# Two-sided staging buffers in a PEER gate stage, and earlier room for the row pools and the first five expert blocks

## The chip, the cores and the metric

One Trainium2 chip, one of its cores. The metric is device time in microseconds (us) of one execution. The engines of the core are TensorE (PE in the rows; PEld is its weight load), VectorE (DVE), ScalarE (ACT), GpSimd (POOL) and SyncE (SP). SP, ACT and POOL also issue DMA transfers; each issues in its own program order, so a transfer that has to wait holds back what stands behind it on that queue.

## The reference

One layer of an encoder on 1024 tokens of width 1024. The part that matters here is its last, a layer of 16384 single-neuron experts:

```python
def one_block(xb):
    ...
    eid = jnp.take_along_axis(cand_i, pos, axis=-1)
    gate = jax.nn.softmax(best_s, axis=-1)
    u = jnp.take(expert_down, eid, axis=0)
    act = jax.nn.gelu(jnp.einsum('thkd,td->thk', u, xb).astype(jnp.float32), approximate=False)
    v = jnp.take(expert_up, eid, axis=0)
    return jnp.einsum('thk,thkd->td', (gate * act).astype(v.dtype), v)
```

Each token chooses 8 x 16 experts; its result is the gated sum of their output rows. Before it stand attention, retention and two projections, behind it a last RMSNorm. All of it is float32; products on PE are made of three passes over operands split in a high and a low part.

## The kernel before

The 1024 tokens are eight tiles of 128. Five tiles (set B) go through **all** 16384 experts as dense products, in 128 blocks of 128 experts; the other three tiles (set A) fetch their chosen experts' rows with indirect DMAs (gathers).

The stages in order of time: attention and retention with the output projection; the choice of experts (to about 893 us); then the **gate stage** (lines 890 to 931); then the **dense stage** (lines 934 to 1160), to the end.

- *The gate stage* turns the choices of each of the five B tiles into a dense table. Per tile and per group of four tokens it builds two one-hot matrices (`oh` on DVE, `bo` on ACT, `ao` mostly on POOL), multiplies them on PE (`pg`), and copies the product into a staging buffer `stg` of 64 KB in each partition (DVE and ACT). Eight DMAs of 1 MB on SP's queue then store a tile's `stg` in `g_dr` in DRAM (line 930), as runs of 512 bytes. Pool `gs` holds two `stg` buffers: tiles 0, 2 and 4 use one, tiles 1 and 3 the other.
- *The dense stage* runs over the 128 blocks. For a block, `ur` (512 KB of `ut`) is loaded and split into `uh` (ACT) and `ul` (DVE) by `split_u`; `products` multiplies them with the five tiles' activations (48 matmuls into `pa`) and ACT applies the GELU (`hf`); `down` multiplies with the block's row of `g_dr` (`gt`) and splits the result into `hh` and `hl`; `up` multiplies these with the halves `vh`, `vl` of the output rows `vr` (30 matmuls into `po` per block) and `add` sums into `acc`.
- *The prologue of the dense stage* (lines 1112 to 1135) does the products of blocks 0 to 4 ahead of everything else: their loads have own buffers `first0` to `first4` in pool `pro`, and their results go to `hfirst0` to `hfirst4`. Later each `first` buffer takes that block's row of `g_dr`. Four gathers stand beside each of these five blocks.
- *The gathers* (`gather_tiles`): POOL issues an indirect DMA of 128 rows of 4 KB (512 KB) into one of five buffers `rows` in pool `gp`, and DVE reduces it against the tile's activations `xng` (line 988). `xng` is loaded over ACT's queue (line 984).

A scheduler orders the instructions of each engine when the program is built; each engine then runs its own in that order. A pool's room can be used by another pool only when every last use of the tiles in it is over. In bytes of a partition, the pools of the two stages lie as follows: `gw` with `gc` (one-hots) 26272 to 52896, `gs` 52896 to 183968 (first buffer to 118432, second from there), and, for the dense stage, `du` (`ur`, `uh`, `ul`, `vr`) 17056 to 44192, `dc` (`acc`) 44192 to 64672, `dw` (`gt`, `hh`, `hl`, `vh`, `vl`) 64672 to 115360, `pro` 122848 to 156128, `gp` 156128 to 185312. So `pro` and `gp` lie over `gs`'s second buffer, `dw` over its first.

```python
stg = pg_.tile([P, P, P], F32, name="stg")
...
for k in range(0, P, 16):
    nc.sync.dma_start(g_dr.rearrange("a b t -> b a t")[:, k:k + 16, i * P:(i + 1) * P], stg[:, k:k + 16])
```

Of the kernel before, what the change touches and what calls it, by code (L numbers as in the profile page):

```python
# [10 lines left out]
F32 = mybir.dt.float32  # L11
# [10 lines left out]
P = 128  # L22
# [3 lines left out]
DC = D // P  # L26
# [7 lines left out]
SETS = {"A": list(range(NT - NG, NT)), "B": list(range(NT - NG))}  # L34
# [6 lines left out]
FIRST = 5  # L41
# [13 lines left out]
def peer_layer(tc, ap, dbg=None):  # L55
    nc = tc.nc
    V, S, G, PE = nc.vector, nc.scalar, nc.gpsimd, nc.tensor
# [19 lines left out]
    with ExitStack() as top:  # L77
# [15 lines left out]
        x1_dr = [dram.tile([P, D], F32, name=f"x1_dr{t}") for t in range(NT)]  # L93
# [27 lines left out]
        with ExitStack() as es:  # L121
# [4 lines left out]
            ps = es.enter_context(tc.tile_pool(name="pm", bufs=1, space=PSUM))  # L126
# [207 lines left out]
            for gi, (half, nm) in enumerate(order):  # L334
# [4 lines left out]
                for c2 in range(DC // 2):  # L339
# [11 lines left out]
                    for k, tt in ks:  # L351
                        c = 2 * c2 + k
# [21 lines left out]
                for tt in range(4):  # L374
                    t = 4 * half + tt
# [20 lines left out]
        with ExitStack() as es:  # L396
# [3 lines left out]
            ps = es.enter_context(tc.tile_pool(name="aps", bufs=2, space=PSUM))  # L400
# [71 lines left out]
            def values(h, out):  # L472
                vt = vts[h]
                po = ps.tile([P, 512], F32, name="avp", bufs=1)
                for j in range(NT):
                    mm3(po, vt[:, 0, j], vt[:, 1, j], ah[j // 4][:, j % 4], al[j // 4][:, j % 4],
                        j == 0, j == NT - 1)
                    if j == 3:
                        yield
                oT = pw.tile([P, 512], F32, name="oT", bufs=1)  # L480
                S.activation(oT, po, AF.Copy)
                out.append(oT)
# [59 lines left out]
            for u in range(-2, len(units) + 1):  # L542
# [13 lines left out]
                if 0 <= u < len(units):  # L556
                    h, g, t = units[u]
# [32 lines left out]
        nB = len(SETS["B"])  # L590
        wB = nB * P
# [60 lines left out]
        with ExitStack() as es:  # L652
            ps = es.enter_context(tc.tile_pool(name="ops", bufs=2, space=PSUM))
# [25 lines left out]
            for u, (nm, i, t) in enumerate(todo):  # L679
# [4 lines left out]
                if u == 1:  # L684
                    first = weights(pw0, 0)
                if last is not None:
                    turned(ps, *last, "otp")
                    if last[0] == "A0":
                        first = first, query(pn, ps, SEGS, *first, ("pq", 1), False)
# [161 lines left out]
        def products(ps, hf, bufs, uh, ul):  # L851
            w = wB // parts
            for r in range(parts):
                cs = slice(r * w, r * w + w)
                pa = ps.tile([P, w], F32, name="pa", bufs=bufs)
                for c in range(DC):
                    mm3(pa, uh[:, c], ul[:, c], nh[:, c, cs], nl[:, c, cs], c == 0, c == DC - 1)
                S.activation(hf[:, cs], pa, AF.Gelu)  # L858
# [3 lines left out]
        with ExitStack() as es:  # L862
            pq_ = {k: es.enter_context(tc.tile_pool(name=f"swq{k}", bufs=1)) for k in (1, 2, 0)}
            pw = es.enter_context(tc.tile_pool(name="sw", bufs=2))
            ps = es.enter_context(tc.tile_pool(name="sps", bufs=2, space=PSUM))
# [23 lines left out]


        g_dr = dram.tile([P, P, wB], F32, name="g_dr")
        with ExitStack() as es:
            pc = es.enter_context(tc.tile_pool(name="gc", bufs=1))
            pw = es.enter_context(tc.tile_pool(name="gw", bufs=4))
            pg_ = es.enter_context(tc.tile_pool(name="gs", bufs=2))
            ps = es.enter_context(tc.tile_pool(name="gps", bufs=2, space=PSUM))
            iop = pc.tile([P, P, 4], BF16, name="iop")
            G.iota(iop, pattern=[[1, P], [0, 4]], base=0, channel_multiplier=0, allow_small_or_imprecise_dtypes=True)
            for i in range(nB):
                pT = ps.tile([P, 3, P], F32, name="gtp")  # L900
                for k in range(3):
                    PE.transpose(pT[:, k], selE[k][:, i].rearrange("p h k -> p (h k)"), ident)
                kT = pw.tile([P, 2, P], BF16, name="kT", bufs=1)
                V.tensor_copy(kT, pT[:, 0:2])
                gT = pw.tile([P, P], F32, name="gT", bufs=1)
                V.tensor_copy(gT, pT[:, 2])
                stg = pg_.tile([P, P, P], F32, name="stg")
                for q in range(0, P, 4):
                    o2 = pw.tile([P, 2, P, 4], BF16, name="oh")
                    V.tensor_tensor(o2, bc(iop[:, None], [P, 2, P, 4]), bc(kT[:, :, None, q:q + 4], [P, 2, P, 4]),  # L910
                                    op=ALU.is_equal)
                    oh = [o2[:, k].rearrange("p n t -> p t n") for k in range(2)]
                    bo = pw.tile([P, 4, P], F32, name="bo")
                    S.activation(bo, oh[1], AF.Copy)
                    ao = pw.tile([P, 4, P], F32, name="ao")
                    if q // 4 % 11:
                        G.tensor_tensor(ao, oh[0], bc(gT[:, q:q + 4, None], [P, 4, P]), op=ALU.mult)  # L917
                    else:
                        for j in range(4):
                            S.activation(ao[:, j], oh[0][:, j], AF.Copy, scale=gT[:, q + j:q + j + 1])  # L920
                    pg = ps.tile([P, 4, P], F32, name="pg", bufs=6)
                    for j in range(4):
                        PE.matmul(pg[:, j], bo[:, j], ao[:, j], start=True, stop=True)  # L923
                    dst, src = stg[:, :, q:q + 4], pg.rearrange("p t a -> p a t")
                    if q // 4 % 5 in (0, 2):
                        V.tensor_copy(dst, src)
                    else:
                        S.activation(dst, src, AF.Copy)
                for k in range(0, P, 16):
                    nc.sync.dma_start(g_dr.rearrange("a b t -> b a t")[:, k:k + 16, i * P:(i + 1) * P], stg[:, k:k + 16])  # L930
        early.close()


        gp = top.enter_context(tc.tile_pool(name="gp", bufs=1, side="right"))
        late = {}

        def tail(t, o):
# [65 lines left out]
        with ExitStack() as es:  # L1003
# [4 lines left out]
            acc = [pc.tile([P, D], F32, name=f"acc{i}") for i in range(nB)]  # L1008
# [21 lines left out]
            def load(a):  # L1030

                if a < P and a not in BEFORE:
                    raw[a] = pu.tile([P, DC, P], F32, name="ur", bufs=1)
                    nc.sync.dma_start(raw[a], ap["ut"][a])
# [10 lines left out]
            def split_u(a):  # L1045
                if a in raw:
                    uh = pu.tile([P, DC, P], F32R, name="uh")
                    ul = pu.tile([P, DC, P], F32R, name="ul")
                    ur = raw.pop(a)
                    S.activation(uh, ur, AF.Copy)  # L1050
                    V.tensor_tensor(ul, ur, uh.bitcast(F32), op=ALU.subtract)  # L1051
                    ready[a] = uh, ul

            def down(a):
                hf, gt = ready.pop(a), gts.pop(a)
                if isinstance(hf, tuple):
                    u, hf = hf, pu.tile([P, wB], F32, name="hf", bufs=1)
                    products(ps, hf, 2, *u)

                mark[0] = V.tensor_tensor(gt, gt, hf, op=ALU.mult).ins  # L1060

                if a >= FIRST:
                    gathers(RATE / 4)
                hh = pd.tile([P, wB], F32R, name="hh", bufs=2 * GB - 1)
                hl = pd.tile([P, wB], F32R, name="hl", bufs=2 * GB - 1)
                S.activation(hh, gt, AF.Copy)
                V.tensor_tensor(hl, gt, hh.bitcast(F32), op=ALU.subtract)
                hs[a] = hh, hl
                if a >= FIRST:
                    gathers(RATE / 4)  # L1070
# [38 lines left out]
                        add(k, t)  # L1109


            with tc.tile_pool(name="pro", bufs=1, side="right") as pp:
                first = [pp.tile([P, DC * P], F32, name=f"first{a}") for a in range(FIRST)]
                for a, ur in enumerate(first):
                    S.dma_start(ur.rearrange("p (c e) -> p c e", e=P), ap["ut"][a])
                load(FIRST)
                for a, ur in enumerate(first):
                    raw[a] = ur.rearrange("p (c e) -> p c e", e=P)
                    split_u(a)
                    ready[a] = ready[a], pp.tile([P, wB], F32, name=f"hfirst{a}")  # L1120
                    products(ps, ready[a][1], 2, *ready[a][0])
                    ready[a] = ready[a][1]
                    for _ in range(4):
                        next(gen)
                split_u(FIRST)
                load(FIRST + 1)
                values(0)
                values(1)
                for a, ur in enumerate(first):
                    gts[a] = ur[:, 0:wB]  # L1130
                    nc.sync.dma_start(gts[a], g_dr[a])
                for t, o in zip(SETS["B"], acc):
                    nc.sync.dma_start(o, x1_dr[t])
                for a in range(FIRST):
                    down(a)
            for a in range(FIRST - 1, P):
                if a >= FIRST:
                    down(a)
# [70 lines left out]
```

## Time and profile before

| | us |
|---|---|
| median of three runs | 3129.86 (3127.61 to 3130.92) |
| the profiled execution | 3130.9 |
| its span, first to last instruction | 3129.1 |
| PE busy in the span | 2850.7 (91%) |
| DVE busy | 2589.1 (83%) |
| POOL busy | 1706.6 (55%) |
| ACT busy | 1071.8 (34%) |

The profile is of one execution; 1.8 us of its time lie outside the span. Times in the rows count from the span's start. Durations of neighbouring matmuls overlap, so a count of matmuls over the time between two starts tells PE's pace better than the sum of their durations. PEclk is the granted clock of PE as a share of full speed; "DMA share" the mean busy share of the 16 DMA engines.

### The profile page before, as it was taken

What the parts mean: (1) busy time and instruction counts of PE and PEld (TensorE: products, weight loads), DVE (VectorE), ACT (ScalarE), POOL (GpSimd) and SP (SyncE); (2) the same over time, 40 slices, a digit from 0 to 9 for tenths busy, and PEclk for the clock granted to TensorE, in tenths of its full rate; (3) what the DMA queues carried; (4) which work ended last, traced back from release to release, by engine and by line L of the source; (5) the groups of instructions that cost most, each with busy time, mean ns of one, the idle gap of its engine ahead of it and who ended that gap; (6) DMA issues with size and microseconds to landing.
All of it is one profiled execution on the core that took longest, in us unless ns stands there. A gap on an engine that the chain in (4) does not pass through costs nothing.

```text
span 3129.1 us, 44717 instructions
## 1 busy us (share of the span) xinstructions
PE 2850.7 (91%) x15999; PEld 2528.5 (81%) x15999; DVE 2589.1 (83%) x4867; ACT 1071.8 (34%) x1750; POOL 1706.6 (55%) x1319
## 2 busy tenths in 40 slices
PE   8999798898978847998899898999999999999998
PEld 6888577798977637887788787898999889998997
DVE  5465587579999946898998888888999988889997
ACT  4444466422247732222223222222222222222222
POOL 3422455346559944666556556565555465655551
PEclk9999899999999978999899999999999999999999
DMA  4334955331006688877777879999999899999994
GB/s 160 110 122 134 197 115 108 123 127 37 23 18 172 176 254 308 304 275 260 280 267 249 279 273 352 330 325 325 341 328 326 298 348 326 328 331 337 330 325 169
DMA packets 327919, 742.54 MB, mean 237 GB/s; under 512 B 25872, under 2 KB 133008, under 8 KB 327696
## 3 DMA queue, kind: packets, MB, share of 16 engines
q0 software_dynamic: 123520, 419.48, 39.2%
q1 hardware_dynamic: 201584, 315.28, 30.7%
q10 hardware_dynamic: 2592, 4.93, 0.5%
q8 instruction: 126, 2.06, 0.3%
q14 instruction: 97, 0.79, 0.1%
HBM read 669.26 MB, written 70.32 MB: 236 GB/s over the span
## 4 chain that ended last, share of the span: by engine, by line
PE 27%; DVE 15%; issue 14%; POOL 8%; DMA 5%; ACT 1%; SPq 1%; POOLq 0%; DVEq 0%; ACTq 0%
POOL rows L978 6%; PE po L73 5%; PE po L75 5%; PE po L74 5%; PE pa L73 4%; PE pa L74 4%; PE pa L75 4%; DVE gacc L997 4%; DVE rows L988 2%; DVE oh L910 2%; DMA rows<-peer_u,idx 2%; DMA ur<-ut 1%; POOL ao L917 1%; DVE acc L1094 1%; SPq L930 1%
## 5 line engine op out<-in xcount | busy, mean ns | idle before, releaser
L978 POOL DMA_INDIRECT rows<-peer_u,idx x384 | 525.8, 1369 | 401.6 <-DVE act L988 236.7
L978 POOL DMA_INDIRECT rows<-peer_v,idx x384 | 470.1, 1224 | 401.7 <-DVE gacc L997 338.4
L73 PE MATMUL pa<-nThB,uh 128*128 128x320 f32 x2048 | 639.0, 312 | 54.4 <-ACT uh L1050 39.4
L75 PE MATMUL pa<-nThB,ul 128*128 128x320 f32 x2048 | 636.0, 311 | 15.3 <-DVE ul L1051 15.3
L74 PE MATMUL pa<-nTlB,uh 128*128 128x320 f32 x2048 | 636.5, 311 | 0.0
L73 PE MATMUL po<-vh,hh 128*128 128x512 f32 x1280 | 516.0, 404 | 66.1 <-DVE acc L1094 65.9
L75 PE MATMUL po<-vh,hl 128*128 128x512 f32 x1280 | 509.6, 398 | 0.0
L74 PE MATMUL po<-vl,hh 128*128 128x512 f32 x1280 | 508.3, 397 | 0.7 <-DVE vl L1083 0.7
L997 DVE SCALAR_TENSOR_TENSOR gacc<-rows,act,gacc 128x1024 f32<-128x1024 f32 x384 | 502.9, 1310 | 5.5 <-DMA rows<-peer_v,idx 4.6
L988 DVE CUSTOM_DVE_ANT_0 rows<-rows,xng 128x1024 f32<-128x1024 f32 x384 | 467.0, 1246 | 44.8 <-DMA rows<-peer_u,idx 30.1
L73 PEld LDWEIGHTS pa<-nThB,uh 128*128 128x128 f32 x2048 | 389.9, 190 | 61.0 <-ACT uh L1050 39.6
L75 PEld LDWEIGHTS pa<-nThB,ul 128*128 128x128 f32 x2048 | 389.7, 190 | 16.6 <-DVE ul L1051 16.0
L74 PEld LDWEIGHTS pa<-nTlB,uh 128*128 128x128 f32 x2048 | 390.0, 190 | 4.4
L73 PEld LDWEIGHTS po<-vh,hh 128*128 128x128 f32 x1280 | 246.8, 193 | 124.5 <-DVE acc L1094 75.1
L1082 ACT ACTIVATE vh<-vr 128x512 fp32r<-128x512 f32 x256 | 160.2, 628 | 384.4 <-PE po L75 168.0
L75 PEld LDWEIGHTS po<-vh,hl 128*128 128x128 f32 x1280 | 246.2, 192 | 55.6
L74 PEld LDWEIGHTS po<-vl,hh 128*128 128x128 f32 x1280 | 246.7, 193 | 49.1 <-DVE vl L1083 1.5
L1050 ACT ACTIVATE uh<-ur 128x1024 fp32r<-128x1024 f32 x118 | 125.2, 1061 | 371.1 <-PE pa L74 199.1
L1051 DVE TENSOR_TENSOR ul<-ur,uh 128x1024 fp32r<-128x1024 f32 x118 | 145.7, 1234 | 102.6 <-ACT uh L1050 67.5
L917 POOL TENSOR_TENSOR ao<-oh,gT 128x512 f32<-128x512 bf16 x145 | 206.9, 1462 | 22.3 <-DVE oh L910 22.3
L923 PE MATMUL pg<-ao,bo 128*128 128x128 f32 x1280 | 181.5, 289 | 41.0 <-POOL ao L917 32.3
L858 ACT ACTIVATE hf<-pa 128x320 f32<-128x320 f32 x246 | 105.7, 430 | 328.4 <-PE pa L75 300.3
(344 smaller groups left out, 5481.3 us busy)
## 6 DMA issues: line engine op xcount, KB each, us to landing
vr<-peer_v SPq DMA_DIRECT2D x256, 256.0 KB
ur<-ut SPq DMA_DIRECT2D x123, 512.0 KB
g_dr<-stg SPq DMA_DIRECT2D x40, 1024.0 KB
gt<-g_dr SPq DMA_DIRECT2D x123, 320.0 KB
wr<-w_in SPq DMA_DIRECT2D x48, 512.0 KB
wqr<-wq SPq DMA_DIRECT2D x32, 576.0 KB
kt<-dk_dr POOLq DMA_DIRECT2D x16, 512.0 KB
xr<-xT SPq DMA_DIRECT2D x24, 256.0 KB
```

What stands on the lines that cost most here:

```text
L73: PE.matmul(out, ah, bh, start=first, stop=False)
L74: PE.matmul(out, ah, bl, start=False, stop=False)
L75: PE.matmul(out, al, bh, start=False, stop=last)
L858: S.activation(hf[:, cs], pa, AF.Gelu)
L917: G.tensor_tensor(ao, oh[0], bc(gT[:, q:q + 4, None], [P, 4, P]), op=ALU.mult)
L923: PE.matmul(pg[:, j], bo[:, j], ao[:, j], start=True, stop=True)
L978: G.indirect_dma_start(out=u, out_offset=None, in_=table, in_offset=bass.IndirectOffsetOnAxis(ap=idx, axis=0))
L988: V.tensor_tensor_reduce(out=u, in0=u, in1=xn, scale=1.0, scalar=0.0, op0=ALU.mult, op1=ALU.add, accum_out=act[:, k:k + 1])
L997: V.scalar_tensor_tensor(o, v, act[:, k:k + 1], o, op0=ALU.mult, op1=ALU.add)
L1050: S.activation(uh, ur, AF.Copy)
L1051: V.tensor_tensor(ul, ur, uh.bitcast(F32), op=ALU.subtract)
L1082: S.activation(vh, vr, AF.Copy)
```

## The change

The two `stg` buffers become two pools of one buffer each: `gs0` on the left at 52896 to 118432 and `gs1` on the right at 119776 to 185312. `gs1` is closed after tile 3 (the last tile that uses it) instead of after tile 4, and the pools `gp` and `pro` are opened at once, inside the loop, together with the loads of the five `first` buffers. Those loads go from ACT's queue to SP's. `pro` is closed where its block ended before. The other pools keep their places. The core of the diff:

```diff
         g_dr = dram.tile([P, P, wB], F32, name="g_dr")
+        pros = ExitStack()
         with ExitStack() as es:
...
-            pg_ = es.enter_context(tc.tile_pool(name="gs", bufs=2))
+
+            odd = ExitStack()
+            pgs = [es.enter_context(tc.tile_pool(name="gs0", bufs=1)),
+                   odd.enter_context(tc.tile_pool(name="gs1", bufs=1, side="right"))]
...
-                stg = pg_.tile([P, P, P], F32, name="stg")
+                stg = pgs[i % 2].tile([P, P, P], F32, name="stg")
...
                 for k in range(0, P, 16):
                     nc.sync.dma_start(g_dr.rearrange("a b t -> b a t")[:, k:k + 16, i * P:(i + 1) * P], stg[:, k:k + 16])
+                if i == (nB - 2 if nB % 2 else nB - 1):
+                    odd.close()
+                    gp = top.enter_context(tc.tile_pool(name="gp", bufs=1, side="right"))
+                    pp = pros.enter_context(tc.tile_pool(name="pro", bufs=1, side="right"))
+                    firsts = [pp.tile([P, DC * P], F32, name=f"first{a}") for a in range(FIRST)]
+                    for a, ur in enumerate(firsts):
+                        nc.sync.dma_start(ur.rearrange("p (c e) -> p c e", e=P), ap["ut"][a])
         early.close()
 
 
-        gp = top.enter_context(tc.tile_pool(name="gp", bufs=1, side="right"))
...
-            with tc.tile_pool(name="pro", bufs=1, side="right") as pp:
-                first = [pp.tile([P, DC * P], F32, name=f"first{a}") for a in range(FIRST)]
-                for a, ur in enumerate(first):
-                    S.dma_start(ur.rearrange("p (c e) -> p c e", e=P), ap["ut"][a])
-                load(FIRST)
...
+            load(FIRST)
...
             for a in range(FIRST):
                 down(a)
+            pros.close()
```

Three places show how the instructions move. First SP's queue at the end of the gate stage; `g_dr<-stg` are the stores (eight a tile, 40 in all), `ur` is the load of block 5, `vr` are output rows, `first<-g_dr` the blocks' rows of the table. Before:

```order
L930 DMA g_dr<-stg 128x16x128 x32
L1034 DMA ur<-ut 128x1024
L930 DMA g_dr<-stg 128x16x128 x8
L1079 DMA vr<-peer_v 128x512 x2
L1133 DMA acc_10827<-x_dr_70 128x1024
```

Now:

```order
L934 DMA g_dr<-stg 128x16x128 x32
L941 DMA first_10405<-ut 128x1024
L941 DMA first_10406<-ut 128x1024
L941 DMA first_10407<-ut 128x1024
L941 DMA first_10408<-ut 128x1024
L941 DMA first_10409<-ut 128x1024
L934 DMA g_dr<-stg 128x16x128 x8
L1044 DMA ur<-ut 128x1024
L1089 DMA vr<-peer_v 128x512 x2
L1137 DMA first_10405<-g_dr 128x640
```

The five loads stand between the stores of tile 3 and those of tile 4, and the load of block 5 has moved from ahead of tile 4's stores to behind them.

Second ACT's order, from the gate stage's last copies on. Before:

```order
L928 ACTIVATE stg<-pg 128x128x4 x3
L1115 DMA first_10835<-ut 128x1024
L1115 DMA first_10836<-ut 128x1024
L1115 DMA first_10837<-ut 128x1024
L1115 DMA first_10838<-ut 128x1024
L1115 DMA first_10839<-ut 128x1024
L1050 ACTIVATE uh<-first_10835 128x1024
L984 DMA xng<-xn_dr_83 128x1024
L1050 ACTIVATE uh<-first_10836 128x1024
L1082 ACTIVATE vh<-vr 128x512 x2
```

Now:

```order
L932 ACTIVATE stg<-pg 128x128x4 x2
L994 DMA xng<-xn_dr_83 128x1024
L932 ACTIVATE stg<-pg 128x128x4
L1060 ACTIVATE uh<-first_10405 128x1024
L1060 ACTIVATE uh<-first_10406 128x1024
L858 ACTIVATE hfirst_10855<-pa 128x320
L1060 ACTIVATE uh<-first_10407 128x1024
```

The load of `xng` is issued ahead of the last copy, the split of block 0 right behind it, and `vh` no longer stands among the first splits.

Third DVE's order from its last copies on; `ISA rows,act` is the reduction of a gather (an `ISA act` behind each reads its sum). Before:

```order
L926 COPY stg<-pg 128x128x4 x2
L1051 TENSOR_TENSOR ul<-first_10835,uh 128x1024
L1051 TENSOR_TENSOR ul<-first_10836,uh 128x1024
L988 ISA rows,act<-rows,xng 128x1024
L988 ISA act 128x1
```

Now:

```order
L930 COPY stg<-pg 128x128x4 x2
L998 ISA rows,act<-rows,xng 128x1024
L998 ISA act 128x1
L1061 TENSOR_TENSOR ul<-first_10405,uh 128x1024
L998 ISA rows,act<-rows,xng 128x1024
L998 ISA act 128x1
L998 ISA rows,act<-rows,xng 128x1024
L998 ISA act 128x1
L1061 TENSOR_TENSOR ul<-first_10406,uh 128x1024
```

Before, two splits stood ahead of the first reduction and eight reductions between the second split and the third; now one reduction stands ahead of the first split, two more ahead of the second, and four, four, five and three ahead of those of blocks 2, 3, 4 and 5. Some 120 DVE instructions further on, and from that place on every engine, the orders before and now are the same.

## Rows read from the trace of the kernel before

**Rows 1.** Stretches: us; PE, PEld, DVE, ACT, POOL busy (count); PEclk; DMA share; GB/s.

```profile
1129.50:1169.00 39.50, 0.07 (x2) 0.06 (x1) 0.07 (x1) 1.65 (x2) 4.16 (x5) 0.56 0.98 291
1169.00:1300.00 131.00, 113.00 (x639) 105.42 (x640) 96.26 (x143) 35.77 (x57) 65.82 (x47) 0.89 0.86 307
...
1700.00:1900.00 200.00, 182.01 (x991) 162.81 (x990) 180.55 (x339) 56.03 (x84) 111.86 (x88) 0.95 0.80 280
1900.00:2100.00 200.00, 191.95 (x1070) 174.67 (x1069) 174.83 (x273) 52.02 (x84) 122.10 (x90) 0.98 0.92 330
...
2900.00:3000.00 100.00, 100.00 (x564) 91.28 (x563) 89.89 (x97) 27.56 (x44) 52.69 (x44) 1.00 0.92 327
```

**Rows 2.** Waits from 1129 to 1230 us: total, times, longest.

```profile
PE pa L73 <- ACT uh L1050: 39.4, 1, 39.4
POOL rows L978 <- DMA vr<-peer_v: 35.3, 1, 35.3
...
PE pa L75 <- DVE ul L1051: 14.7, 1, 14.7
```

**Rows 3.** The chain that ended last, across the gap: start, us, what.

```profile
1151.56 10.80 DMA g_dr<-stg
...
1162.75 4.69 DMA first<-ut
...
1170.57 16.77 DMA xng<-xn_dr
```

**Rows 4.** SP's queue in order of time: start, us, what was issued.

```profile
1087.59 24.40 SPq L930 DMA_DIRECT2D g_dr<-stg  x8
...
1130.17 24.96 SPq L930 DMA_DIRECT2D g_dr<-stg  x8
1155.17 5.17 SPq L1079 DMA_DIRECT2D vr<-peer_v  x2
```

**Rows 5.** Short stretches around the gap, columns as in rows 1.

```profile
1112.00:1121.00 9.00, 7.59 (x56) 6.67 (x56) 9.00 (x10) 7.80 (x16) 8.31 (x7) 1.00 0.71 197
1121.00:1130.00 9.00, 7.01 (x51) 5.84 (x49) 6.69 (x8) 5.07 (x9) 7.30 (x6) 1.00 0.00 1
1130.00:1140.00 10.00, 0.00 (x0) 0.00 (x0) 0.00 (x0) 0.14 (x1) 0.00 (x0) 0.71 0.96 288
...
1190.00:1200.00 10.00, 0.00 (x0) 0.00 (x0) 7.03 (x13) 0.00 (x0) 8.17 (x7) 0.50 0.73 234
```

**Rows 6.** PE in order of time; in brackets the idle time before.

```profile
1168.95 0.63 PE L73 MATMUL pa<-nThB,uh 128*128 128x320 f32 x1 [39.43 <-ACT uh L1050]
1201.16 0.63 PE L75 MATMUL pa<-nThB,ul 128*128 128x320 f32 x1 [14.70 <-DVE ul L1051]
...
1224.79 0.40 PE L73 MATMUL po<-vh,hh 128*128 128x512 f32 x1
```

**Rows 7.** DVE in order of time: first reduction, then the splits of blocks 2 and 5.

```profile
1187.48 1.22 DVE L988 CUSTOM_DVE_ANT_0 rows<-rows,xng 128x1024 f32<-128x1024 f32 x1 [13.94 <-DMA xng<-xn_dr]
...
1199.89 1.22 DVE L1051 TENSOR_TENSOR ul<-first,uh 128x1024 fp32r<-128x1024 f32 x1
...
1222.95 1.22 DVE L1051 TENSOR_TENSOR ul<-ur,uh 128x1024 fp32r<-128x1024 f32 x1
```

**Rows 8.** POOL in order of time: its last gate work, the first gather.

```profile
1118.52 9.78 POOL L917 TENSOR_TENSOR ao<-oh,gT 128x512 f32<-128x512 bf16 x7
1163.62 1.08 POOL L978 DMA_INDIRECT rows<-peer_u,idx  x1 [35.32 <-DMA vr<-peer_v]
```

**Rows 9.** DMA queues, 1085 to 1163 us: packets, MB, share of 16 engines.

```profile
q1 hardware_dynamic: 33400, 17.74, 81.2%
```

**Rows 10.** DMA queues, 1163 to 1300 us: q0 POOL, q1 SP, q10 ACT.

```profile
q0 software_dynamic: 6624, 24.12, 50.0%
q1 hardware_dynamic: 5368, 14.98, 30.7%
q10 hardware_dynamic: 864, 3.15, 5.8%
```

More of the change, by code (lines that the diff above doesn't have):

```diff
@@ L1109, in up @@
                         add(k, t)
-            with tc.tile_pool(name="pro", bufs=1, side="right") as pp:
-                first = [pp.tile([P, DC * P], F32, name=f"first{a}") for a in range(FIRST)]
-                for a, ur in enumerate(first):
-                    S.dma_start(ur.rearrange("p (c e) -> p c e", e=P), ap["ut"][a])
-                load(FIRST)
[L1117 to L1135, printed above, removed]
+            load(FIRST)
+            for a, ur in enumerate(firsts):
+                raw[a] = ur.rearrange("p (c e) -> p c e", e=P)
+                split_u(a)
+                ready[a] = ready[a], pp.tile([P, wB], F32, name=f"hfirst{a}")
+                products(ps, ready[a][1], 2, *ready[a][0])
+                ready[a] = ready[a][1]
+                for _ in range(4):
+                    next(gen)
+            split_u(FIRST)
+            load(FIRST + 1)
+            values(0)
+            values(1)
+            for a, ur in enumerate(firsts):
+                gts[a] = ur[:, 0:wB]
+                nc.sync.dma_start(gts[a], g_dr[a])
+            for t, o in zip(SETS["B"], acc):
+                nc.sync.dma_start(o, x1_dr[t])
+            for a in range(FIRST):
+                down(a)
+            pros.close()
             for a in range(FIRST - 1, P):
```

## The prediction, made before the change was run

> **What bounds the kernel now.** I read the busy time by stretch first, then the waits across the gap it shows, then the chain, then the DMA queues.
>
> From 1129.5 to 1169 us, PE, DVE, ACT and POOL do next to nothing while the DMA engines are 98% busy [rows 1]: the gap is tile 4's eight stores. They are issued from 1130.17 on [rows 4] and the last lands at 1151.56 + 10.80 = 1162.4 [rows 3]. Everything of the dense stage that lies over `gs` waits for that: PE for the first split 39.4 us, POOL for its first gather 35.3 us [rows 2]; the wait that the view puts down to `vr` is the stores', since the gather starts at 1163.62 [rows 8]. A second stall follows: `xng` takes 16.77 us behind the five `first` loads in ACT's queue [rows 3], so DVE's first reduction is at 1187.48, the split of block 2, eight reductions behind it, at 1199.89 [rows 7], and PE stands 14.7 us [rows 2, 6]. The first `po` matmul, after the five blocks' products, starts at 1224.79 [rows 6]. From 1900 us on PE is bound: 96% busy from 1900 to 2100, 100% from 2900 to 3000, with DMA at 0.92 [rows 1]. So what the start gains is kept to the end: past the prologue every engine's order is the same in both kernels, and the gathers' pace is tied to the blocks'.
>
> **The change part by part.** *The release.* Tile 3's stores are issued until 1112 [rows 4] and run out in the stretch to 1121; from there to 1130 the DMA engines stand still [rows 5]. So `gs1` is free by about 1120, ahead of tile 4's end. The two buffers themselves cost nothing: each tile keeps the buffer that it had, and a whole tile of gates still lies between a buffer's uses.
>
> *The five first loads* go on SP's queue behind tile 3's stores. SP waits there until about 1120, and what is queued behind are tile 4's stores, not due before 1130.17: nothing is delayed. The loads are five sixths of the 3.15 MB that took 5.8% of 137 us on q10 [rows 10], 6.6 us; they run in the empty stretch [rows 5] and are there by 1130. ACT loses five issues, off the path now.
>
> *PE's start.* The split of block 0 follows the last `stg` copy, which ends as the stores begin (1130.17) [rows 4]; with about 1 us for the split, PE starts near 1131.3 instead of 1168.95 [rows 6]: 37.6 us earlier. But it runs only the passes that need no `ul`. DVE now has one reduction ahead of the first `ul`, and that waits for `xng` and a gather, both issued at about 1128.3, when POOL ends its gate work [rows 8]. This added wait has no row. Lower bound: `xng` alone, 0.52 MB at q1's 30.7% x 137 / 14.98 = 2.8 us per MB [rows 10], 1.5 us; upper: 16.77 us, as in the old queue [rows 3]. The five loads are no longer ahead of it, so I take 8 us, nearer the lower end: `ul` of block 0 at about 1139, a stall of 6 us where the old one was 14.7. PE's clock, 0.50 in the old stall [rows 5], that is 1.2 of 2.4 GHz, may fall for part of it; the fall stood in the old start too.
>
> *The new limit.* The first `po` now needs all of this over the DMA engines, from 1130.2 on: tile 4's stores, because `dw` (`hh`, `vh`) lies over `gs0`; the load of block 5, behind them on SP; and 19 gathers, because DVE has 19 reductions ahead of block 5's split. Prices: stores, 81.2% of 78 us for 17.74 MB [rows 9], so 8.39 MB (eight of 1 MB) take 29.9 us. Gathers, 50.0% of 137 us for 24.12 MB [rows 10], so 1.49 us per 0.524 MB: 19 take 28.3 us. Block 5, `xng`, two `vr` and three rows of `g_dr`, 2.6 MB at 2.8 us: 7 us. Sum 65 us, done at 1195 with engines that never idle; behind block 5's load come its two splits and the short steps to `hh`, some 6 us as an estimate from the 1.22 us of a split [rows 7]. So `po` starts near 1201, 24 us before 1224.79. PE, with five products to do, isn't the bound.
>
> *From there to 1300.* I ask the same of all work that the old kernel had done at 1300. DMA time from 1163 to 1300: 50.0 + 30.7 + 5.8 = 86.5% of 137 us, 118.5 us [rows 10]; less the first loads' 6.6, plus the stores' 29.9, makes 141.8 us to do from 1130.2 on. At a share of 1, as in the gap [rows 1], it is done at 1272 (28 us gained); at 0.92, as where PE is bound [rows 1], at 1284 (16 us gained). The middle is 22 us, and `po`'s 24 agrees. From 1700 to 1900 the DMA share is 0.80 [rows 1], so no further loss follows; deeper gaps there, by the order of DVE, move along unchanged. Moved `acc` loads and the later `vr` splits lie in the same sum.
>
> *The added wait on SP.* Block 5's load moves behind eight stores, 25 us of issue [rows 4]. It was needed late then (split at 1222.95 [rows 7]) and is in the sum now. Nothing else is queued past.
>
> *A rule beside it.* In the trace a store's packet takes 81.2% x 78 x 16 / 33400 = 30 ns [rows 9] and a gather's 50.0% x 137 x 16 / 6624 = 166 ns [rows 10]. If the queues take turns by these packets, the stores get 30/196 = 15% of the engines while gathers wait: they end after the gathers and the load behind them comes last, so that all 65 us are served and 24 rather than 19 gathers stand ahead, 5 x 1.49 = 7 us more: `po` near 1208, a gain of 17 us. If they share by bytes, the stores end first and the sum above holds. The Trainium skill, "DMA: Bandwidth & Descriptors", section "Queues, rings and completion order", says that an engine goes round its queues packet by packet, a packet being several descriptors. By that rule the gain is 17 us if the trace's packets are meant, 24 if bundles of like size are; no row here shows which.
>
> **The sum.** -22 us: 3130.9 of the profiled execution becomes 3109. That execution is 1.0 us over the median, so 3108 beside 3129.86.
>
> **The rivals.**
> - *DMA does not limit; the gap is won whole.* For: the stores run at 288 GB/s [rows 5], the loads and gathers behind them at 307 with engines only 86% busy [rows 1], so writes and reads together may move more than either. Then the reductions set the pace: 20 of them from 1187.48 to the split at 1222.95 [rows 7], 1.77 us each; 19 from about 1137 end at 1171, `po` starts near 1177, 48 us gained: 3083. Against: a share of 0.98 in the gap [rows 1] leaves stores and gathers little to overlap. Half of it, 35 us, gives 3096.
> - *Turns by packet, as above*: the stores last; 17 us gained, 3114.
> - *Small writes and large reads slow each other.* Place: from 1130 until the stores have landed, on which `hh`, `vh` and block 5 wait. Each us that they land later than the plan costs one. No change is reached when `po` starts at 1225, that is when the 65 us become 89 (37% more); slower by over 0.2% from 96 us on. At 100 us `po` starts at 1236: 3142. For: one 16.77 us transfer of 0.52 MB [rows 3]. Against: that one stood behind the five loads.
> - *The release doesn't happen:* loads and gathers still wait for tile 4, nothing changes, 3131. SP's order speaks against it, since there the loads stand ahead of tile 4's stores.
>
> **How the numbers follow.** Forecast (12 to 30 us gained) 0.60; won whole or half (over 30) 0.17; turns by packet, down to 7 us gained, 0.12; no release or the slowdown up to its zero 0.08; slower 0.03. The range leaves out gains over 38 us and under 8 us: 3092 to 3122. A measurement of this kernel can tell about 0.2%, 6 us, from no change. Faster by more than that: 0.60 + 0.17 + 0.11 = 0.88; same 0.09; slower 0.03.
>
> **What would show it.** Right: the `first` loads land before 1130; PE starts at 1131 to 1132, stalls some us for `ul`; the DMA share stays over 0.95 from 1130 to 1200; `po` starts near 1201; the tail of the trace is the old one moved by some 22 us. Wrong: `po` near 1177 (DMA was no limit), or a stall of PE over 14.7 us for the first `ul`, or stores landing after 1200, or a gap from 1300 on that the old kernel didn't have.

## The result and the profile after

| | before | changed |
|---|---|---|
| median of four runs each, us | 3128.74 | 3098.85 |
| lowest and highest, us | 3122.45, 3130.92 | 3088.40, 3099.38 |
| the profiled execution, us | 3130.9 | 3088.4 |
| its span, us | 3129.1 | 3086.6 |

The ratio is 0.990, with a 95% interval of 0.9874 to 0.9925: 30 us less by the medians, 23 to 39 us by the interval. The forecast was 3108, in a range of 3092 to 3122, so 22 us less by the profiled execution. One execution of the kernel before, in the set of e9 to e12 below, took 4190.5 us at a granted clock of 0.61; it is left out of every figure here.

The two profiled executions lie 42 us apart, and 7.1 us of that isn't the change's: the first store of tile 4 is issued at 1130.17 us in the one [rows 4] and at 1123.07 in the other, and all runs of the study lie between 1121.5 and 1130.9 there, the unchanged stages ahead of it being what differs (the first `oh` of the gate stage starts at 905.6 in the one and at 898.4 in the other). So from here on times are counted **from the first store of tile 4** (S). By that count the first `po` came at 94.6 before and comes at 63.75 now, 30.9 us earlier; the end came at 1998.9 and comes at 1963.5, 35.4 earlier.

SP's queue of the changed kernel in order of time (start, us, what was issued), which answers to [rows 4]:

```profile
1111.85 2.40 SPq L941 DMA_DIRECT2D first<-ut  x5
1123.07 51.48 SPq L934 DMA_DIRECT2D g_dr<-stg  x8
1174.66 3.27 SPq L1044 DMA_DIRECT2D ur<-ut  x1
```

The five first loads are issued 11 us ahead of tile 4's stores. The stores' issue now takes 51.5 us instead of 25, and block 5's load comes after it. PE in order of time, which answers to [rows 6]:

```profile
1124.04 0.42 PE L73 MATMUL pa<-nThB,uh 128*128 128x320 f32 x1 [1.63 <-ACT uh L1060]
1130.11 0.63 PE L75 MATMUL pa<-nThB,ul 128*128 128x320 f32 x1 [5.22 <-DVE ul L1061]
...
1183.18 0.64 PE L73 MATMUL pa<-nThB,uh 128*128 128x320 f32 x1 [16.04 <-ACT hfirst L858]
...
1186.82 0.80 PE L73 MATMUL po<-vh,hh 128*128 128x512 f32 x1 [0.47 <-ACT hh L1076]
```

PE starts at S + 1.0 instead of + 38.8, stands 5.2 us for the first `ul`, runs through its five products, and then stands 16.0 us that weren't there before. ACT, in order of time, tells why:

```profile
1159.32 0.44 ACT L858 ACTIVATE hfirst<-pa 128x320 f32<-128x320 f32 x1 [3.08 <-PE pa L75]
1181.75 1.06 ACT L1060 ACTIVATE uh<-ur 128x1024 fp32r<-128x1024 f32 x1 [21.99 <-DMA ur<-ut]
1182.71 0.42 ACT L858 ACTIVATE hfirst<-pa 128x320 f32<-128x320 f32 x1
```

ACT waits 22 us for block 5's load, the one that moved behind the stores; the GELU of block 4, whose data were long there, stands behind that split in ACT's order, and PE's next product behind the GELU. This stall isn't what the first `po` waits for, though. The chain of work that ended last, in order of time (start, us, what), leads to it over another transfer of SP's queue:

```profile
1179.00 4.99 DMA first<-g_dr
...
1186.03 0.75 ACT hh L1076
```

The row of `g_dr` for block 0 is issued behind the stores, block 5's load and two `vr`, lands at 1183.99, and DVE and ACT make `hh` of it; PE is idle for 0.47 us more for that `hh` and then starts `po`. The chain has no wait for the landing of the stores in it, only their place in the queue. Short stretches of the changed kernel, columns as in [rows 1]:

```profile
1130.00:1140.00 10.00, 9.89 (x58) 9.90 (x59) 8.68 (x15) 1.82 (x3) 7.05 (x6) 0.84 1.06 398
1140.00:1150.00 10.00, 10.00 (x70) 10.00 (x69) 6.81 (x11) 2.26 (x4) 5.11 (x5) 1.00 1.06 401
...
1170.00:1180.00 10.00, 0.00 (x0) 0.00 (x0) 0.00 (x0) 0.00 (x0) 0.00 (x0) 0.53 1.12 348
```

The gap of 39 us in which only the DMA engines worked has become one of some 16 us, and while PE works ahead of it the engines move about 400 GB/s, where they moved 288 in the old gap [rows 5].

### The profile page after: what moved, and what is told of

It reads as the page before. It is cut to its first block, busy times and chain, and to the rows that moved or that the text cites. A ratio compares the mean times of both kernels' runs of the same rounds, so it can differ in the third digit from the quotient of the medians.

```text
span 3086.6 us, 44714 instructions
## 1 busy us (share of the span) xinstructions
PE 2841.6 (92%) x15999; PEld 2519.5 (82%) x15999; DVE 2586.1 (84%) x4867; ACT 1072.1 (35%) x1750; POOL 1699.0 (55%) x1319
## 4 chain that ended last, share of the span: by engine, by line
PE 20%; issue 18%; DVE 14%; POOL 11%; DMA 5%; SPq 2%; ACT 2%; POOLq 0%; DVEq 0%; ACTq 0%
POOL rows L988 9%; PE po L73 4%; PE po L75 3%; PE po L74 3%; DVE gacc L1007 3%; PE pa L73 3%; PE pa L74 3%; PE pa L75 3%; DVE rows L998 3%; DVE oh L914 2%; DMA ur<-ut 2%; SPq L934 2%; DMA rows<-peer_u,idx 2%; POOL ao L921 1%; DVE acc L1104 1%
## 5 line engine op out<-in xcount | busy, mean ns | idle before, releaser
L988 POOL DMA_INDIRECT rows<-peer_u,idx x384 | 518.6, 1351 | 348.5 <-DVE act L998 227.2
L73 PE MATMUL po<-vh,hh 128*128 128x512 f32 x1280 | 514.5, 403 | 64.8 <-DVE acc L1104 64.0
L998 DVE CUSTOM_DVE_ANT_0 rows<-rows,xng 128x1024 f32<-128x1024 f32 x384 | 469.7, 1252 | 38.7 <-DMA rows<-peer_u,idx 38.5
```

What stands on the lines that cost most here:

```text
L73: PE.matmul(out, ah, bh, start=first, stop=False)
L988: G.indirect_dma_start(out=u, out_offset=None, in_=table, in_offset=bass.IndirectOffsetOnAxis(ap=idx, axis=0))
L998: V.tensor_tensor_reduce(out=u, in0=u, in1=xn, scale=1.0, scalar=0.0, op0=ALU.mult, op1=ALU.add, accum_out=act[:, k:k + 1])
```

## The experiments

The theory: the first `po` is released by the landing of tile 4's stores and what is queued behind them, and the stores share the DMA engines with the gathers. The rivals: PE's early start is the gain whatever comes behind it; stores and gathers don't disturb each other; the early gathers alone bring it. All edits are against the changed kernel. "First po" and "end" are read from the profiled execution of each run and counted from its own S, as is the end of the stores' issue; the medians are of all timed executions. The sets run together are e1 to e4, e5 to e8 and e9 to e12.

| run | median us | ratio to before, 95% | stores issued until | first po | end |
|---|---|---|---|---|---|
| before | 3126.5 to 3128.8 | 1 | 25.0 | 94.6 | 1998.9 |
| changed | 3098.85 | 0.9900 (0.9874 to 0.9925) | 51.5 | 63.75 | 1963.5 |
| e1, same | 3094.92 | 0.9905 (0.9887 to 0.9922) | 51.7 | 64.0 | 1963.4 |
| e9, same | 3097.55 | 0.9910 (0.9892 to 0.9929) | 52.1 | 64.8 | 1968.9 |
| e2, block 5 over ACT | 3095.29 | 0.9910 (0.9893 to 0.9927) | 53.0 | 64.5 | 1968.8 |
| e3, first loads late | 3133.15 | 1.0017 (1.0003 to 1.0032) | 53.0 | 106.2 | 2001.1 |
| e4, no gathers | 3094.48 | 0.9904 (0.9888 to 0.9920) | 28.7 | 43.3 | 1968.3 |
| e5, stores twice | 3125.93 | 0.9990 (0.9979 to 1.0001) | 81.0 | 95.6 | 1997.4 |
| e6, two gathers | 3087.76 | 0.9879 (0.9862 to 0.9895) | 40.7 | 53.6 | 1957.4 |
| e10, two gathers | 3090.22 | 0.9885 (0.9867 to 0.9903) | 40.6 | 54.2 | 1960.0 |
| e7, two, 6.1 a block | 3087.53 | 0.9875 (0.9858 to 0.9892) | 39.5 | 53.6 | 1956.5 |
| e8, none, 6.2 a block | 3101.21 | 0.9920 (0.9906 to 0.9934) | 28.4 | 42.9 | 1965.9 |
| e11, first loads over ACT | 3110.64 | 0.9951 (0.9937 to 0.9966) | 56.9 | 71.8 | 1978.2 |
| e12, two, block 5 over ACT | 3098.97 | 0.9911 (0.9895 to 0.9928) | 41.0 | 53.8 | 1966.3 |

**The spread (e1, e9).** No edit.

> The changed kernel once more, nothing edited: how far its executions lie apart. Both theories: 3098 to 3100 us in most executions, some 29 us (0.9%) under the kernel before; the one at 3088.4 that was profiled stays rare. From the start of the last tile's stores to the first po matmul about 64 us (before: 94.6).

> The changed kernel again, beside the next runs on the same chip. Both theories: 3094 to 3100 us, 1963 to 1964 us from the last tile's first store to the end.

The medians of the same program in three sets lie 4 us apart (3094.92 to 3098.85), the end behind S 5.5 us. Both expectations were too narrow: e1's executions lie from 3089 to 3101 us, not mostly at 3098 to 3100, and e9's end is 1968.9 us behind S, not 1963 to 1964. A few us between two runs of the table are no finding.

**First loads late (e3).** The row pools keep the early room; pool `pro` lies over tile 4's buffer, and its loads go over ACT's queue again:

```diff
-                    pp = pros.enter_context(tc.tile_pool(name="pro", bufs=1, side="right"))
-                    firsts = [pp.tile([P, DC * P], F32, name=f"first{a}") for a in range(FIRST)]
-                    for a, ur in enumerate(firsts):
-                        nc.sync.dma_start(ur.rearrange("p (c e) -> p c e", e=P), ap["ut"][a])
...
+            pp = pros.enter_context(tc.tile_pool(name="pro", bufs=1))
+            firsts = [pp.tile([P, DC * P], F32, name=f"first{a}") for a in range(FIRST)]
+            for a, ur in enumerate(firsts):
+                S.dma_start(ur.rearrange("p (c e) -> p c e", e=P), ap["ut"][a])
             load(FIRST)
```

> The row pools keep the early room, but the five first buffers lie over the last tile's staging buffer and are loaded over ACT's queue after its stores, as before: the gathers start in the gap, PE does not. Theory (the gap was worth what PE's five products and the gathers could both do in it; with stores slowed by the gathers the first loads land 55 to 60 us after the stores' start): first po 95 to 105 us after the stores' start, time 3120 to 3135, nothing of the gain left. Rival (early gathers alone bring the gain, since the old stall of 14.7 us behind xng goes): first po at 75 to 80 us, time 3110 to 3115.

PE in order of time:

```profile
1197.38 0.63 PE L73 MATMUL pa<-nThB,uh 128*128 128x320 f32 x1 [67.17 <-ACT uh L1056]
```

Nothing of the gain is left, as the theory said, if a little later than it said (first `po` at 106.2, expected 95 to 105): the gathers run in the gap, the stores are issued for 53 us, and PE, whose first loads now wait for them, starts at S + 66.5 instead of + 38.8. The early gathers alone are worth nothing; they even delay PE by 28 us. Since DVE has all twenty reductions behind it by then, the first `po` is only 12 us later than before and the end 2 us. The edit changes the loads' queue as well as their room; e11 below changes the queue alone and costs 13 us, so about 13 of the 37.6 us between this run and the changed kernel (S to the end) may be the queue's.

**Stores twice (e5).**

```diff
                     nc.sync.dma_start(g_dr.rearrange("a b t -> b a t")[:, k:k + 16, i * P:(i + 1) * P], stg[:, k:k + 16])
+                    if i == nB - 1:
+                        nc.sync.dma_start(g_dr.rearrange("a b t -> b a t")[:, k:k + 16, i * P:(i + 1) * P], stg[:, k:k + 16])
```

> The last tile's eight stores are each issued twice, so 16.8 MB instead of 8.4 MB leave in the place where PE waits. Theory (the first po is released by the landing of these stores and of the load queued behind them): first po 84 to 96 us after the stores' start instead of 64, time 3115 to 3128. Rival (PE's early start is the gain and the rest is made up): time within 8 us of the changed kernel's 3095 to 3099.

PE starts early all the same (S + 1.0), and yet the first `po` comes at 95.6 and the whole gain is gone. So the rival is out: PE's early start alone keeps nothing, and what counts is when the stores are done. Whether that means landed, or only through SP's queue so that the loads behind them can be issued, this run doesn't tell apart. (The second store of each pair also waits for the first, 38.7 us of waits in SP's queue in all, so the 29 us added to the issue are not the price of the bytes.)

**No gathers beside the first blocks (e4), and more of them later (e8).**

```diff
-                for _ in range(4):
-                    next(gen)
```

e8 has `RATE = 6.2` as well, instead of 6.0.

> No gathers beside the first five blocks; they come later, all 20 of them. Theory (the engines serve stores and gathers from one purse): stores land 32 to 36 us after their start instead of some 55, first po at 42 to 46 us instead of 64; the 20 gathers are then missing at the end, where each costs its 1.2 to 1.5 us, so the time is 3092 to 3106. Rival (stores and gathers do not disturb each other): first po stays at 60 us or more.

> No gathers beside the first five blocks, and 6.2 a block later. Theory: first po at 43 us, and without the late gathers at the end 1950 to 1962 us after the stores' start, against 1968.4 with 6.0 a block. If DVE binds the middle: 1965 or more.

The stores' issue, as SP's queue shows it in e4:

```profile
1124.35 28.65 SPq L934 DMA_DIRECT2D g_dr<-stg  x8
```

Four gathers still run at the start, where the changed kernel has 24. The stores take 28.7 us to issue, nearly the old 25, and the first `po` comes at 43.3: twenty gathers hold the stores back by 23 us and the first `po` by 20. But the end is no earlier. POOL's last gather is the sign: in e4 it is issued at

```profile
3062.31 0.95 POOL L988 DMA_INDIRECT rows<-peer_v,idx  x1 [3.18 <-DVE gacc L1007]
```

30 us before the end of the span (3092.7), in the changed kernel at

```profile
3032.61 1.15 POOL L988 DMA_INDIRECT rows<-peer_v,idx  x1 [2.44 <-DVE gacc L1007]
```

54 us before it (3086.6). So e4 ends with the gathers that were put off. e8 spreads them over the blocks: its last gather is issued at 3032.07, 60 us before the end of its span (3092.5), so its end no longer waits for them. Yet it wins only 2.4 us behind S in the profile and none in the median; the expectation that it would reach 1950 to 1962 was wrong. From the first `po` to the end it takes 1923.0 us, e4 1925.1, the changed kernel 1899.8: the twenty gathers cost some 19 to 25 us wherever they were put (e9: 1904.1). 1965.9 is what was set down for a middle bound by DVE, but that it is DVE is not shown by more than this number.

**Two gathers a block (e6, e10), and 6.1 later (e7).**

```diff
-                for _ in range(4):
+                for _ in range(2):
                     next(gen)
```

e7 has `RATE = 6.1` as well.

> Two gathers instead of four beside each of the first five blocks, ten of them later. Theory (one purse for stores and gathers, and a gather served later costs something only where it makes the end late): first po 50 to 56 us after the stores' start, between the 43 us without gathers and the 64 us with twenty; time 1957 to 1966 us after the stores' start (changed kernel: 1963.5). Rival (no disturbance): first po at 60 us or more.

> The kernel with two gathers beside each of the first five blocks, repeated next to the changed kernel. Theory: 5 to 10 us under it, 3086 to 3092 us, 1957 to 1958 us from the first store to the end. If the gain seen before was the chip's: within 2 us of it.

> As the run with two gathers, and 6.1 instead of 6.0 gathers a block later, which makes up for the ten left out. Theory: the end no longer waits for gathers, 1953 to 1962 us after the stores' start, 2 to 10 us under the changed kernel. If the middle of the dense stage is bound by DVE, the added gathers cost there what they save at the end: 1963 or more.

SP's queue in e6, and PE's first `po`:

```profile
1126.95 40.74 SPq L934 DMA_DIRECT2D g_dr<-stg  x8
```

```profile
1180.56 0.80 PE L73 MATMUL po<-vh,hh 128*128 128x512 f32 x1 [0.48 <-ACT hh L1076]
```

Between none and four, as expected: 40.7 us of issue, first `po` at 53.6. Here the ten gathers that come later cost less than the 10 us that the first `po` gains. Both sets put this kernel ahead of the changed one: 3087.8 and, beside it in one set, 3090.2 against 3097.55. **By the medians it beats both kernels of this case**, the one before by 36 to 41 us, the changed one by 7. In e10 the end is 1960.0 us behind S, where 1957 to 1958 was expected. Against the changed kernel the lead is little more than the spread: the intervals of e9 and e10 overlap (0.9892 to 0.9903), but the timed executions of e6, e7 and e10 lie from 3083 to 3092 us, those of the changed program from 3088 to 3107. The added 6.1 of e7 makes no difference that can be told.

**Block 5's load over ACT's queue (e2, e12).**

```diff
-            def load(a):
+            def load(a, queue=None):
...
-                    nc.sync.dma_start(raw[a], ap["ut"][a])
+                    (queue or nc.sync).dma_start(raw[a], ap["ut"][a])
...
-            load(FIRST)
+            load(FIRST, S)
```

e12 has two gathers a block as well.

> Block 5's load goes over ACT's queue instead of behind the eight stores on SP's. Theory (the first po waits for the stores to land, and PE idles there only because block 5's load lands behind them): the load lands within 15 us of its issue, PE's idle stretch before the first po shrinks from some 24 us by the 7 us of one block's product, and the time falls by 4 to 8 us against the changed kernel (3091 to 3095). Rival (PE's early start is the whole gain, the stall behind it is made up later): within 2 us of the changed kernel.

> Two gathers a block, and block 5's load over ACT's queue. In the order, the first po stands ahead of block 5's products then, so that they no longer fill the wait. Theory: first po 50 to 55 us after the stores' start, time within 4 us of the kernel with two gathers alone. Rival (the load behind the stores holds PE): 5 us or more faster than that kernel.

PE's first `po` in e2:

```profile
1189.18 0.80 PE L73 MATMUL po<-vh,hh 128*128 128x512 f32 x1 [18.75 <-DMA ur<-ut]
```

A miss: with the load early, the scheduler put the first `po` ahead of block 5's products in PE's order (240 `pa` matmuls stand ahead of it, 249 in the changed kernel), so the idle stretch was not filled. e2's 3095.29 us is that of the unchanged program in the same set (3094.92), which is what the rival had set down; but e5 speaks against that rival. What the two runs do show is that block 5's load doesn't hold the first `po`, which stays where it was without it (64.5; 53.8 in e12). The name behind the wait, `ur`, can't be right for `po`, which reads no `ur`; PEld's wait for the same matmul names `hh` (19.0 us), and the chain goes from SP's queue over a `vr`, issued behind the stores and landed at 1186.25, to `vh`, `vl`, `hh` and `po`. e12 is 9 us slower than e10 in the same set, where at most 4 was expected; PE has done 13 us less work by S + 1900 in it, spread over several stretches. Why stays open.

**First loads over ACT's queue (e11).**

```diff
-                        nc.sync.dma_start(ur.rearrange("p (c e) -> p c e", e=P), ap["ut"][a])
+                        S.dma_start(ur.rearrange("p (c e) -> p c e", e=P), ap["ut"][a])
```

> The five first loads go back to ACT's queue, at the same place in the program; the order then puts two splits ahead of the first reduction and eight reductions between the second split and the third, as in the kernel before, and xng behind the five loads. Theory (stores and gathers set the first po, not PE's five products): PE starts without waiting for the first reduction but stands longer before block 2, and the first po comes 62 to 70 us after the stores' start, time within 6 us of the changed kernel. Rival (the queue and the order it brings are part of the gain): first po at 75 us or more, 10 us slower or worse.

Waits in e11 from S to S + 110 (engine and line waited for, total us, times, longest):

```profile
ACT vh L1092 <- DMA g_dr<-stg: 18.1, 1, 18.1
...
PE pa L73 <- ACT hfirst L858: 14.0, 1, 14.0
PE pa L75 <- DVE ul L1061: 13.7, 3, 13.1
```

The theory's figures were missed: first `po` at 71.8, 13 us slower than e9 beside it, closer to the rival. PE waits 2.8 us for the first split, so the loads are there nearly in time; what changes most is the order that comes with them. DVE has eight reductions ahead of block 2's split again (13.1 us of PE's), and ACT has `vh`, whose room is tile 4's buffer, ahead of GELUs that PE waits for (14.0 us). The loads also come later: ACT issues them from S - 3.8, where SP issued them from S - 11.2, so that 1.7 of their 2.6 MB now move beside the stores, whose issue takes 56.9 us instead of 52.1. The run doesn't tell the order from the later issue. Together about 13 of the 30 us hang on the loads' queue. The run shows the stores' landing, too: `vh` is released by it at 1191.7, S + 63.

## Why the prediction was right, and what was sized wrong

- **The release, the first loads, PE's start: right.** Loads out before S, PE at S + 1.0 (forecast + 1.1), the stall for the first `ul` 5.2 us (forecast 6). e3 shows that without the early loads nothing of the gain is left. "ACT loses five issues, off the path now" put at nothing what was worth 13 us: the queue itself, by e11.
- **The new limit: right in kind.** The first `po` waits for tile 4's stores and for loads queued behind them, not for PE; e5 moves it by 32 us with stores alone, e4 and e6 by 20 and 10 with gathers alone. But the load is not that of block 5, which the forecast had on the path: moved to another queue in e2 and e12, it leaves the first `po` where it was, and the chains name block 0's row of `g_dr` and `vr`. Nor are the reductions the limit, although 19 of them stood in the forecast: DVE is through with all of them at 1165.5 and waits 17.3 us for block 5's `uh`. A stall of PE before the first `po`, which the sum implied, is there: 16 us. That ACT's order would put a finished block's GELU behind the late load wasn't seen.
- **The sum of 65 us: the term that was sized wrong.** "Done at 1195 with engines that never idle" added prices taken from stretches in which stores and gathers ran apart. Together they took less. Queues of the changed kernel, 1133 to 1163 us (packets, MB, share of 16 engines):

```profile
q0 software_dynamic: 2192, 8.00, 65.3%
q1 hardware_dynamic: 7399, 3.76, 41.5%
```

and of the kernel before, from 1135 to 1160 us, stores alone:

```profile
q1 hardware_dynamic: 14407, 7.32, 104.4%
```

  Alone: 7.32 MB in 25 us, 293 GB/s. Together: 11.8 MB in 30 us, 393 GB/s, with shares that add up to 107%. At the sum's prices these bytes come to 8.00 x 1.49 / 0.524 + 3.76 x 29.9 / 8.39 = 36 us, so the prices were 20% too high. A gather's packet took 65.3% x 30 us x 16 / 2192 = 143 ns (166 in the sum), a store's 41.5% x 30 us x 16 / 7399 = 27 ns (30 in the sum). That it is the mixing which makes them cheaper is not shown, since stores alone don't have one price. In the changed kernel, from 1172 to 1179 us, behind the last gather:

```profile
q1 hardware_dynamic: 4668, 2.40, 115.7%
```

  This is 343 GB/s without any gathers, 28 ns a packet. Block 5's load was there at S + 58.7 and the first row of `g_dr` at S + 60.9, although 24 gathers had been issued by then, two of them just ahead of S, where 19 were priced. With five more the sum would have been 72 us. So 65 came nearer than its terms deserved, by luck: too few gathers and too high prices partly cancelled. The first `po` came 7 us earlier than forecast (63.75 against 70.8), and that is about the 8 us by which the gain was too small in the forecast (22 us; 30 by the medians, the upper end of the 12 to 30 of the likeliest case).
- **From there to the end: right.** From the first `po` to the end it is 1904.3 us before, 1899.4 to 1904.1 in three executions of the changed kernel, 1904.3 in e2, 1901.8 in e5, 1903.7 and 1905.8 in e6 and e10. What the start gains is kept. It is longer without the twenty early gathers (1925.1 in e4, 1923.0 in e8) and in e12 (1912.5), and shorter in e3 (1894.9); for these two the cause stays open.
- **The turns.** If an engine served one packet of the trace from each queue in turn, the stores would have got 15% of its time. They got 41.5 / 106.8 = 39%, 3.4 packets for each of the gathers'. The Trainium skill, "DMA: Bandwidth & Descriptors", "Queues, rings and completion order", speaks of turns by packets that hold several descriptors; the trace agrees as far as that more than one 512-byte run is served for one packet of a gather. How many of either make one turn it doesn't show, and the 39% are those of the rule only if both queues had work all the time (15 gathers issued in the 30 us, 7.5 us each to landing, so near four under way in the mean). Turns by single packets of the trace are out, if so. But what that rival drew from them came true, and the forecast's "the stores end first" did not: the last of the 24 gathers is issued at 1165.26, the stores until 1174.55, with all 24 ahead of block 5's load. It missed only the time, since everything together took less than priced.
- **The other rivals.** Won whole (first `po` near S + 47): not so, though e4, without the twenty gathers, comes to 43. Small writes and large reads slow each other: not so, the two together took less than priced. No release: SP's queue shows that the room was free, with the loads issued 11 us ahead of S.

## What to carry to other kernels

When a wait for room is taken away at a stage's border, ask next which transfer the following stage needs last, what stands ahead of it in its queue, and what else will now share the DMA engines with it: here a wait of 39 us was taken from PE, and 31 of them reached the first `po`, because the stores had to share with twenty gathers; halving those early gathers brought about 7 us more, little over the spread. A load that moves behind a row of large stores on one queue can hold up finished work on another engine, by the order of that engine alone; whether that costs time is another question: here the first `po` waited for something else, and what PE's idle stretch cost behind it is not shown. And when prices of transfers are added, take them from a stretch in which the same kinds run together; apart, they came out 20% too high here.

## What the runs showed that was not expected

- Stores to DRAM in runs of 512 bytes and gathers of 4 KB rows together moved 393 GB/s for 30 us, where the prices read apart give 36 us for the same bytes. Stores alone moved 293 GB/s in one stretch and 343 in another.
- Twenty gathers of 0.52 MB lengthened the issue of eight 1 MB stores from 28.7 to 51.5 us, ten to 40.7.
- The same five loads on another queue cost 13 us, although PE waited only 2.8 us for the first of them, by the order of instructions that the scheduler built around them and by their later issue; the two aren't told apart.
